# One tile for the high and the low part of x, gate and up matmuls by high weights first, and attention heads in larger units

## The chip, the cores and the metric

The kernel runs on 1 core of one Trainium2 chip. The metric is the device time of one execution in microseconds (us); lower is better. Each time given for a kernel is a median over runs. A profiled execution has a time of its own and a trace: every instruction of TensorE (PE, with its weight loads as PEld), VectorE (DVE), ScalarE (ACT) and the DMA queues, with start and duration.

## What is computed

Three transformer blocks one after the other on x of 256 tokens by 1024, all in fp32: a first block with a mixer of dilated attention and RWKV-7, then a block of two layers with a mixer of three kinds of attention. Every block or layer has a feed-forward half step before and after its mixer, so there are six of these. Cut to what the change touches:

```python
x = x + 0.5 * swiglu_2(rmsnorm(x, ffn1_norm), ffn1_w_gate, ffn1_w_up, ffn1_w_down)
h = rmsnorm(x, mix_norm) @ w_in
...
o_a = chunk_relpos_attention(hd4(a_q, A_HEADS), hd4(a_k, A_HEADS), hd4(a_v, A_HEADS), a_rel_bias)   # 6 heads of 64
o_b = dsa_attention(...)                                                                             # 5 heads of 64
o_c = mla_attention(...)                                                                             # 5 heads, q and k of 96, v of 64
x = x + jnp.concatenate([o_a, o_b, o_c], axis=-1) @ w_out
x = x + 0.5 * swiglu_2(rmsnorm(x, ffn2_norm), ffn2_w_gate, ffn2_w_up, ffn2_w_down)

def swiglu_2(x, w_gate, w_up, w_down):                    # 1024 -> 2816 -> 1024
    return (jax.nn.silu(x @ w_gate) * (x @ w_up)) @ w_down
```

## The kernel before

Nine parts run in order: f0, m1, f1 (the first block), f2, n0, f3 and f4, n1, f5 (the two layers). `f` is a feed-forward (`ffn`), `m1` the first mixer (`mixer1`), `n` a mixer of the second kind (`mixer2`).

**Numbers in two parts.** PE multiplies fp32 in a rounded form here (float32r). So that no accuracy is lost, each operand is split into a high part, which is the value rounded to that form, and a low part, which is the rest: `xh`, `xl` for x, `hi`, `lo` for weights. A product is then three matmuls: low weight by high x, high weight by high x, high weight by low x. A weight chunk of 128 by 1024 is loaded by DMA from the SP queue into `raw` (512 KB); ACT makes `hi` from it (L361), DVE makes `lo` (L362). `split` (L376, L377) does the same for other tiles.

**Feed-forward.** The 2816 hidden columns are 11 pieces of 256 (`NP`). Piece 0 has code of its own (`first`). For pieces 1 to 10, `gu(p)` computes gate and up: the weights are stationary (128 by 128), x is moving, the results are four PSUM banks of 128 by 256 (two halves `c` of gate, two of up; tags `gu`, `gu` and `tr0`, `tr1`). For each of 8 slices k of x and each of the four banks there are three matmuls of 256 columns, L557 to L559. So a group is 96 matmuls; all four banks end together at k = 7. DVE then multiplies each bank by `rrow`, the factor of the norm laid out along the columns (L565, L567), ACT takes silu (L566), DVE multiplies the two (L568), and `split` makes `hh` and `hl`. `down(p-1)` follows: 24 matmuls (L370 to L372) with `hh` or `hl` as stationary and 512 columns of the down weights as moving, into the banks y0 to y3. After group 9 no `down` stands: group 10 follows it directly.

**Heads in mixer2.** `heads` computes attention for a set of heads in units: a unit is one of the two query blocks (`qt`) with 3 or 4 heads at `qt` 0 and 1 or 2 at `qt` 1, so that a unit's scores fill one bank. A unit goes through three steps, each a step behind the unit before: `softmax` (scores by L1247, mask or bias, row maximum, exponentials with their sums), `turned` (128 by 128 transposes of the exponentials, L1265) and `values` (L1277: the transposed exponentials are stationary, 64 columns of v are moving; DVE divides by the sums, L1278 and L1279, and writes `o`). Later `ready` transposes `o` (L1420, 16 transposes in a mixer) and splits it for the output projection. There are three calls: the six heads of kind A, the five of C, the five of B. `weave` lays other work, which is mostly projections, between their steps.

**What sets the order.** The code issues instructions in the order of these loops; the framework's scheduler then lays them out per engine before the run, and each engine runs its list strictly in that order, waiting where a semaphore says so. Buffers are pools: in a feed-forward `hi`, `lo` and (from piece 2 on) `raw` have six buffers each, which six chunks a group (four of gate and up, two of down) use in turn.

Rows of the scheduled order are shown below as `line operation out<-in size`; `ps_gu`, `ps_tr0`, `ps_y` are PSUM banks by tag.

Of the kernel before, what the change touches and what calls it, by code (L numbers as in the profile page):

```python
# [9 lines left out]
F32 = mybir.dt.float32  # L10
F32R = mybir.dt.float32r
# [289 lines left out]
class Kern:  # L301
# [143 lines left out]
    def prep(self, t, gain, normed):  # L445
# [33 lines left out]
    def ffn(self, f, end):  # L479

        nc, tc = self.nc, self.tc
        with tc.tile_pool(name="ffn%d" % f, bufs=2, reuse_waits="tile") as pool:
            t2 = lambda name: pool.tile([128, 512], F32, name=name, tag="t2", bufs=12)
            self.begin(pool, t2, "f%d" % f)
            xh, xl = self.xh, self.xl
            y, hT, wd = [], [None] * NP, [None] * NP
# [15 lines left out]
            def first():  # L502
# [4 lines left out]
                for t in range(2):  # L507
# [11 lines left out]
                    nc.vector.scalar_tensor_tensor(h, ps[t][:, 256:], rs, sg, op0=OP.mult, op1=OP.mult)  # L519
# [25 lines left out]
            def gu(p):  # L545

                mm = nc.tensor.matmul
                ps = [[self.bank(tag)[:, :256] for tag in tags]
                      for tags in (("gu", "gu"), ("y2", "y3") if p == 1 else ("tr0", "tr1"))]
# [21 lines left out]
            hs, rrow = first(), []  # L571
            for p in range(1, NP):
# [7 lines left out]
            for t in range(2):  # L580
# [652 lines left out]
    def heads(self, tt, groups, qk, scores, scale, vap, o, h0, tags=("y0", "y1"), tags2=("y2", "y3")):  # L1233
# [3 lines left out]
        units = [(qt, g[i:i + 4 // (qt + 1)]) for qt in range(2) for g in groups  # L1237
# [326 lines left out]
```

## Time and profile before

| | |
|---|---|
| time, median of 3 runs | 1838.87 us (1837.1 to 1839.02) |
| the profiled execution's own time | 1841.12 us |
| its span, from first to last instruction | 1839.3 us |
| PE busy | 1819.5 us (99%) |
| PEld busy (weight loads, beside the matmuls) | 1660.0 us (90%) |
| DVE busy | 1214.9 us (66%) |
| ACT busy | 918.8 us (50%) |
| DMA | 302.53 MB, mean 164 GB/s |

Busy times of PE hold a trap: a matmul's duration in the trace goes from its start until its last result is written, and the next one starts long before that. How fast PE really goes through a list is read from starts: the start of one row to the start of the next. Shares of busy time say which engine is never without work; they do not say what an instruction costs.

### The profile page before, as it was taken

To read this page: it belongs to the slowest core of one execution; us is meant where nothing else is said; L and a number is where in the kernel's file an instruction comes from. 1 tells how busy PE (TensorE), PEld (TensorE's weight loads), DVE (VectorE), ACT (ScalarE), POOL (GpSimd) and SP (SyncE) were. 2 spreads that over 40 slices of the span, in tenths; PEclk is the share of its full clock that TensorE was granted. 3 is DMA by queue.
4 is the path that set the end of the run, shared out by engine and by line. 5 is a ranking of instruction groups with operands and counts; after the bars stand their busy time and mean duration, and the time that the engine had idled before them with its cause. 6 is when DMAs were issued, how large, how long until landed. Compare 5 with 4: busy or idle time off the path is not lost.

```text
span 1839.3 us, 31177 instructions
## 1 busy us (share of the span) xinstructions
PE 1819.5 (99%) x12404; PEld 1660.0 (90%) x12404; DVE 1214.9 (66%) x2214; ACT 918.8 (50%) x1535; POOL 0.2 (0%) x4
## 2 busy tenths in 40 slices
PE   8999999999999999999999999999999999999998
PEld 6999887999998999999998888999899988979997
DVE  6656668955667765585568667656666667666565
ACT  5544476542244544364435766444454446755443
POOL 0000000000000000000000000000000000000000
PEclk9999999999999999999999999999999999999999
DMA  8754335450146856286524337763575434347551
GB/s 273 268 185 135 121 128 142 132 160 19 35 144 200 304 196 190 74 291 200 188 74 137 121 122 260 240 187 116 200 244 179 142 104 136 119 148 250 185 182 47
DMA packets 103076, 302.53 MB, mean 164 GB/s; under 512 B 24721, under 2 KB 26897, under 8 KB 102930
## 3 DMA queue, kind: packets, MB, share of 16 engines
q1 hardware_dynamic: 102210, 298.37, 49.9%
q8 instruction: 97, 1.59, 0.3%
q10 hardware_dynamic: 720, 2.16, 0.3%
q14 instruction: 49, 0.40, 0.1%
HBM read 298.40 MB, written 2.10 MB: 163 GB/s over the span
## 4 chain that ended last, share of the span: by engine, by line
PE 96%; DVE 2%; ACT 1%; DMA 1%; issue 1%; ACTq 0%; DVEq 0%
PE ps_y L370 8%; PE ps_y L371 8%; PE ps_y L372 8%; PE ps_gu L557 6%; PE ps_gu L559 6%; PE ps_gu L558 6%; PE ps_tr L557 6%; PE ps_tr L558 6%; PE ps_tr L559 6%; PE ps_gu L370 4%; PE ps_gu L372 4%; PE ps_gu L371 4%; PE ps_gu L615 3%; PE ps_gu L617 3%; PE ps_gu L616 3%; PE ps_y L1247 1%
## 5 line engine op out<-in xcount | busy, mean ns | idle before, releaser
L362 DVE TENSOR_TENSOR lo<-raw,hi 128x1024 fp32r<-128x1024 f32 (+3 forms) x559 | 661.3, 1195 | 386.6 <-ACT hi L361 384.8
L361 ACT ACTIVATE hi<-raw 128x1024 fp32r<-128x1024 f32 (+3 forms) x559 | 568.2, 1032 | 420.2 <-PE ps_tr L559 167.4
L557 PE MATMUL ps_gu<-xh,lo 128*128 128x256 f32 x960 | 272.6, 284 | 0.4 <-DVE lo L362 0.4
L559 PE MATMUL ps_gu<-xl,hi 128*128 128x256 f32 x960 | 271.6, 283 | 0.0
L558 PE MATMUL ps_gu<-xh,hi 128*128 128x256 f32 x960 | 271.6, 283 | 0.0
L557 PE MATMUL ps_tr<-xh,lo 128*128 128x256 f32 x864 | 244.5, 283 | 0.0
L558 PE MATMUL ps_tr<-xh,hi 128*128 128x256 f32 x864 | 244.5, 283 | 0.0
L559 PE MATMUL ps_tr<-xl,hi 128*128 128x256 f32 x864 | 244.5, 283 | 0.0
L370 PE MATMUL ps_y<-lo,hh 128*128 128x512 f32 x528 | 206.5, 391 | 0.0
L372 PE MATMUL ps_y<-hi,hl 128*128 128x512 f32 x528 | 206.1, 390 | 0.3 <-DVE hl L377 0.3
L371 PE MATMUL ps_y<-hi,hh 128*128 128x512 f32 x528 | 206.1, 390 | 0.0
L557 PEld LDWEIGHTS ps_gu<-xh,lo 128*128 128x128 f32 x960 | 184.0, 192 | 3.6 <-DVE lo L362 0.8
L558 PEld LDWEIGHTS ps_gu<-xh,hi 128*128 128x128 f32 x960 | 184.0, 192 | 2.1
L559 PEld LDWEIGHTS ps_gu<-xl,hi 128*128 128x128 f32 x960 | 184.0, 192 | 0.0
L559 PEld LDWEIGHTS ps_tr<-xl,hi 128*128 128x128 f32 x864 | 165.9, 192 | 0.0
L558 PEld LDWEIGHTS ps_tr<-xh,hi 128*128 128x128 f32 x864 | 165.9, 192 | 0.0
L557 PEld LDWEIGHTS ps_tr<-xh,lo 128*128 128x128 f32 x864 | 165.9, 192 | 0.0
L372 PEld LDWEIGHTS ps_y<-hi,hl 128*128 128x128 f32 x528 | 99.1, 188 | 21.6 <-DVE hl L377 0.7
L370 PE MATMUL ps_gu<-lo,xh 128*128 128x384 f32 (+3 forms) x336 | 116.6, 347 | 0.0
L370 PEld LDWEIGHTS ps_y<-lo,hh 128*128 128x128 f32 x528 | 99.4, 188 | 18.8
L371 PEld LDWEIGHTS ps_y<-hi,hh 128*128 128x128 f32 x528 | 99.3, 188 | 18.5
L372 PE MATMUL ps_gu<-hi,xl 128*128 128x384 f32 (+3 forms) x336 | 113.0, 336 | 0.2 <-DVE xl L377 0.2
(406 smaller groups left out, 3136.8 us busy)
## 6 DMA issues: line engine op xcount, KB each, us to landing
raw<-in_w SPq DMA_DIRECT2D x492, 512.0 KB, 4.1
raw<-in_w SPq DMA_DIRECT2D x32, 384.0 KB, 3.2
raw<-in_w SPq DMA_DIRECT2D x14, 480.0 KB, 3.6
row<-in_norms SPq DMA_DIRECT2D x24, 256.0 KB, 6.8
raw<-in_w SPq DMA_DIRECT2D x10, 320.0 KB, 2.8
raw<-in_w SPq DMA_DIRECT2D x4, 492.0 KB, 6.0
raw<-in_w ACTq DMA_DIRECT2D x3, 512.0 KB, 6.9
bm<-in_bias SPq DMA_DIRECT2D x2, 768.0 KB, 5.6
```

The costliest lines, as they stand in the source:

```text
L361: nc.scalar.activation(hi[:, :w], raw[:, :w], AF.Copy)
L362: nc.vector.tensor_tensor(lo[:, :w], raw[:, :w], hi[:, :w].bitcast(F32), op=OP.subtract)
L370: mm(out, ah, bl, start=start, stop=False)
L371: mm(out, ah, bh, start=False, stop=False)
L372: mm(out, al, bh, start=False, stop=stop)
L557: mm(ps[i][c], wl[:, s], xh[:, k], start=k == 0, stop=False)
L558: mm(ps[i][c], wh[:, s], xh[:, k], start=False, stop=False)
L559: mm(ps[i][c], wh[:, s], xl[:, k], start=False, stop=k == 7)
L615: mm(ps, wl[:, s], xh, start=start, stop=False)
L616: mm(ps, wh[:, s], xh, start=False, stop=False)
L617: mm(ps, wh[:, s], xl, start=False, stop=stop)
L1247: T.matmul(ps[:, j], q[:, qt * 128:qt * 128 + 128], k[:, :nk], start=True, stop=True)
```

## The change

It has three parts.

1. `xh` and `xl` become the two halves of one tile `xx`, so that for a slice k both lie side by side as 512 columns (`x2`).
2. In `gu`, one matmul of 512 columns (L560 of the changed kernel) takes the place of the two with the high weights; it fills the whole bank, high x on the left and low x on the right. All 32 of these come first; then, bank by bank, eight matmuls of 256 columns with the low weights (L569) are added to the left half. As soon as a bank is through, ACT copies its right half out (L571) and DVE adds the left one (L572). The factor `rrow` now multiplies gate alone (L574); up stays without it, and `down`'s result gets the factor per token with the 0.5 instead (`half`).
3. In `heads`, units hold up to six heads. Even heads' scores go to one bank and odd heads' to another, issued in turn. The exponentials are divided by their sums before the transposes (a reciprocal, then one DVE instruction a head, L1285 and L1287). `values` has v as stationary (64 columns) and the transposed exponentials as moving (128 columns), so that the result is already transposed, two heads to a bank column (partitions 0 to 63 and 64 to 127). It is split straight into `mh` and `ml`; `o`, its DVE multiply and `ready` are gone.

```diff
-            self.xh = self.cst.tile([128, 8, 256], F32R, name="xh")
-            self.xl = self.cst.tile([128, 8, 256], F32R, name="xl")
+            self.xx = self.cst.tile([128, 8, 2, 256], F32R, name="xx")
+            self.xh, self.xl = self.xx[:, :, 0], self.xx[:, :, 1]
...
+            x2 = self.xx.rearrange("p k m t -> p k (m t)")
...
-                    nc.vector.scalar_tensor_tensor(h, ps[t][:, 256:], rs, sg, op0=OP.mult, op1=OP.mult)
+                    nc.vector.tensor_tensor(h, ps[t][:, 256:], sg, op=OP.mult)
...
+                low = []
                 for k in range(8):
                     if k % 2 == 0:
                         wh, wl = self.chunk(("gu", f, p, k // 2), pool, deep=pool if p > 1 else None)
+                        low.append(wl)
                     for i in range(2):
                         for c in range(2):
                             o = (k % 2) * 512 + i * 256 + c * 128
-                            s = slice(o, o + 128)
-                            mm(ps[i][c], wl[:, s], xh[:, k], start=k == 0, stop=False)
-                            mm(ps[i][c], wh[:, s], xh[:, k], start=False, stop=False)
-                            mm(ps[i][c], wh[:, s], xl[:, k], start=False, stop=k == 7)
+                            nc.tensor.matmul(ps[i][c], wh[:, o:o + 128], x2[:, k], start=k == 0, stop=False)
...
                 for c in range(2):
                     g, u = (pool.tile([128, 256], F32, name=n) for n in ("g", "u"))
-                    nc.vector.tensor_tensor(g, ps[0][c], rrow[0], op=OP.mult)
-                    nc.scalar.activation(g, g, AF.Silu)
-                    nc.vector.tensor_tensor(u, ps[1][c], rrow[0], op=OP.mult)
+                    for z, i in ((g, 0), (u, 1)):
+                        for k in range(8):
+                            o = (k % 2) * 512 + i * 256 + c * 128
+                            nc.tensor.matmul(ps[i][c][:, :256], low[k // 2][:, o:o + 128], xh[:, k], start=False,
+                                             stop=k == 7)
+                        nc.scalar.activation(z, ps[i][c][:, 256:], AF.Copy)
+                        nc.vector.tensor_tensor(z, ps[i][c][:, :256], z, op=OP.add)
+                        if z is g:
+                            nc.vector.tensor_tensor(g, g, rrow[0], op=OP.mult)
+                            nc.scalar.activation(g, g, AF.Silu)
                     nc.vector.tensor_tensor(u, u, g, op=OP.mult)
                     self.split(hh[:, c], hl[:, c], u)
...
+            nc.vector.tensor_scalar(half, self.rs, 0.5, None, op0=OP.mult)
...
-                    nc.vector.scalar_tensor_tensor(self.x[:, t, s], y[t][h], 0.5, self.x[:, t, s],
+                    nc.vector.scalar_tensor_tensor(self.x[:, t, s], y[t][h], half[:, t:t + 1], self.x[:, t, s],
...
+            for j in range(max(map(len, sides))):
+                for e in range(2):
+                    if j < len(sides[e]):
+                        q, k = qk(sides[e][j])
+                        T.matmul(ps[e][:, j], q[:, qt * 128:qt * 128 + 128], k[:, :nk], start=True, stop=True)
...
+            V.reciprocal(st[:, 1, :n], st[:, 1, :n])
+            for j in range(n):
+                V.tensor_scalar(sb[:, j], sb[:, j], st[:, 1, j:j + 1], None, op0=OP.mult)
...
+                    for h in mine:
+                        r = slice(odd(h) * 64, odd(h) * 64 + 64)
+                        T.matmul(ps[r, x], vap(kt, h), pt[:, order.index(h) * (qt + 1) + kt], start=kt == 0, stop=kt == qt)
...
+                self.split(mh[r0:r1, y:y + n, qs], ml[r0:r1, y:y + n, qs], ps[r0:r1, x:x + n])
...
-            weave(self.heads(tt, [[0, 2, 4], [1, 3, 5]], halves(aT), sc_a, 1.0, v_of(z["av"]), o, 0), fill, 1, 2, 1)
+            weave(self.heads(tt, [(0, [0, 1, 2, 3, 4, 5]), (1, [0, 1, 2, 3]), (1, [4, 5])], halves(aT), sc_a, 1.0,
+                             v_of(z["av"]), 0, at, mh, ml), fill, 1, 2, 1)
```

The calls for C and B change in the same way: units of five heads, four and one. Three places of the scheduled order follow.

PE, in the first feed-forward, at the start of group 10 before (1824 to 1827 are its four banks):

```order
L557 MATMUL ps_gu_1824<-xh_83,lo_1831 128x256
L558 MATMUL ps_gu_1824<-xh_83,hi_1830 128x256
L559 MATMUL ps_gu_1824<-xl_84,hi_1830 128x256
L557 MATMUL ps_tr0_1826<-xh_83,lo_1831 128x256
L558 MATMUL ps_tr0_1826<-xh_83,hi_1830 128x256
L559 MATMUL ps_tr0_1826<-xl_84,hi_1830 128x256
```

PE, a whole group of the changed kernel, its last slice k of the high weights and then the low ones:

```order
L560 MATMUL ps_gu<-xx,hi 128x512 x2
L560 MATMUL ps_tr_409<-xx,hi 128x512
L560 MATMUL ps_tr_410<-xx,hi 128x512
L569 MATMUL ps_gu<-xx,lo 128x256 x8
L569 MATMUL ps_tr_409<-xx,lo 128x256 x8
L569 MATMUL ps_gu<-xx,lo 128x256 x8
L569 MATMUL ps_tr_410<-xx,lo 128x256 x8
L370 MATMUL ps_y_367<-lo,hh 128x512
```

What moved: three matmuls a bank and slice became two, and the low ones, which led each slice, now end the group bank by bank.

DVE, in the first feed-forward, the end of group 9 before (1678 to 1681 are its four banks; `lo_1975` is a low tile of a chunk that comes after):

```order
L565 TENSOR_TENSOR g_1804<-ps_gu_1678,rrow_342 128x256
L567 TENSOR_TENSOR u_1805<-ps_tr0_1680,rrow_342 128x256
L565 TENSOR_TENSOR g_1812<-ps_gu_1679,rrow_342 128x256
L568 TENSOR_TENSOR u_1805<-u_1805,g_1804 128x256
L567 TENSOR_TENSOR u_1813<-ps_tr1_1681,rrow_342 128x256
L362 TENSOR_TENSOR lo_1975<-raw_1972,hi_1974 128x1024
L377 TENSOR_TENSOR hl_1803<-u_1805,hh_1802 128x256
L568 TENSOR_TENSOR u_1813<-u_1813,g_1812 128x256
```

DVE, the end of the same place in the changed kernel, where group 10 follows group 9 with no `down` between (1471 to 1474 are group 9's banks; `lo_1626` belongs to group 10 and takes the buffer of a low tile that group 9 reads until its last bank):

```order
L572 TENSOR_TENSOR g_1533<-ps_gu_1471,g_1533 128x256
L574 TENSOR_TENSOR g_1533<-g_1533,rrow_295 128x256
L572 TENSOR_TENSOR u_1534<-ps_tr0_1473,u_1534 128x256
L576 TENSOR_TENSOR u_1534<-u_1534,g_1533 128x256
L362 TENSOR_TENSOR lo_1626<-raw_1623,hi_1625 128x1024
L377 TENSOR_TENSOR hl_1532<-u_1534,hh_1531 128x256
L572 TENSOR_TENSOR g_1560<-ps_gu_1472,g_1560 128x256
L572 TENSOR_TENSOR u_1561<-ps_tr1_1474,u_1561 128x256
```

What moved: a bank is now emptied by an addition with a copy of its other half, and a weight split stands between the first two banks and the last two.

PE, in n0, the first scores of kind A and what follows until the first transpose of exponentials, before:

```order
L1247 MATMUL ps_y_11008<-qk 128x128 x3
L1247 MATMUL ps_y_11043<-qk 128x128 x3
L1374 MATMUL ps_tr_11055<-ident,cq 128x128 x2
L1247 MATMUL ps_y_11082<-qk 128x256 x2
L370 MATMUL ps_gu<-lo,c_hi 128x480
...
L1265 MATMUL ps_tr_11069<-ident,sm_s 128x128 x2
```

and now:

```order
L1264 MATMUL ps_y_10230<-qk 128x128
L1264 MATMUL ps_y_10231<-qk 128x128
...
L1414 MATMUL ps_tr_10273<-ident,cq 128x128 x2
L370 MATMUL ps_gu<-lo,c_hi 128x480
L371 MATMUL ps_gu<-hi,c_hi 128x480
L1264 MATMUL ps_y_10287<-qk 128x256 x2
L1264 MATMUL ps_y_10288<-qk 128x256
L1414 MATMUL ps_tr_10280<-ident,cq 128x128 x2
L1264 MATMUL ps_y_10288<-qk 128x256
...
L1294 MATMUL ps_tr_10325<-ident,sm_s 128x128
```

What moved: even and odd heads take turns in the first unit; in the second (256 columns) two of one side stand together, and a transpose stands before the last. Between the last score of the first unit and its first transpose stand 13 matmuls of 480 columns, six scores of 256 columns and three pairs of `cq` transposes.

## Rows read from the trace of the kernel before

**Rows 1.** The page, busy time of PE, DVE and ACT, share of the span, instructions.
```profile
PE 1819.5 (99%) x12404; PEld 1660.0 (90%) x12404; DVE 1214.9 (66%) x2214; ACT 918.8 (50%) x1535; POOL 0.2 (0%) x4
```
**Rows 2.** The page, the chain that ended last, by engine.
```profile
PE 96%; DVE 2%; ACT 1%; DMA 1%; issue 1%; ACTq 0%; DVEq 0%
```
**Rows 3.** Groups by line and form: count, busy us, mean ns, idle before.
```profile
L557 PE MATMUL ps_gu<-xh,lo 128*128 128x256 f32 x960 | 272.6, 284 | 0.4 <-DVE lo L362 0.4
```
**Rows 4.** Timeline of PE in f0: start us, duration us, engine, line, operation.
```profile
90.76 0.28 PE L559 MATMUL ps_tr<-xl,hi 128*128 128x256 f32 x1
90.88 0.40 PE L370 MATMUL ps_y<-lo,hh 128*128 128x512 f32 x1
...
91.81 0.39 PE L371 MATMUL ps_y<-hi,hh 128*128 128x512 f32 x1
...
96.12 0.39 PE L372 MATMUL ps_y<-hi,hl 128*128 128x512 f32 x1
96.34 0.28 PE L557 MATMUL ps_gu<-xh,lo 128*128 128x256 f32 x1
```
**Rows 5.** Groups by line and form: DVE and ACT in the feed-forward.
```profile
L362 DVE TENSOR_TENSOR lo<-raw,hi 128x1024 fp32r<-128x1024 f32 x495 | 599.5, 1223 | 370.2 <-ACT hi L361 368.7
L361 ACT ACTIVATE hi<-raw 128x1024 fp32r<-128x1024 f32 x495 | 513.4, 1054 | 388.8 <-PE ps_tr L559 167.4 <-issue 102.5 <-PE ps_y L372 56.3
...
L565 DVE TENSOR_TENSOR g<-ps_gu,rrow 128x256 f32<-128x256 f32 x120 | 49.9, 416 | 0.0
```
**Rows 6.** Busy time of each engine over 37 us of f0, PEclk, DMA share, GB/s.
```profile
97.00:134.00 37.00, 37.00 (x267) 35.08 (x267) 22.39 (x30) 16.67 (x22) 0.00 (x0) 1.00 0.55 176
```
**Rows 7.** Timeline of PE in n0, scores, transposes and projections.
```profile
1025.58 1.26 PE L1247 MATMUL ps_y<-qk 64*128 64x128 f32 x12
1026.77 0.44 PE L1374 MATMUL ps_tr<-ident,cq 128*128 128x128 f32 x2
1027.16 1.13 PE L1247 MATMUL ps_y<-qk 64*128 64x256 f32 x4
1028.22 0.49 PE L370 MATMUL ps_gu<-lo,c_hi 128*128 128x480 f32 x1
...
1028.54 0.38 PE L371 MATMUL ps_gu<-hi,c_hi 128*128 128x480 f32 x1
1028.76 0.38 PE L370 MATMUL ps_gu<-lo,c_hi 128*128 128x480 f32 x1
```
**Rows 8.** Timeline of PE in n0, an idle wait and the values.
```profile
1033.22 0.70 PE L1247 MATMUL ps_y<-qk 64*128 64x256 f32 x2 [0.52 <-DVE sm_s L1433]
...
1035.15 0.78 PE L1277 MATMUL ps_y<-av,sm_p 128*128 128x64 f32 x6
1035.74 0.46 PE L370 MATMUL ps_gu<-lo,c_hi 128*128 128x480 f32 x1
```
**Rows 9.** Timeline of PE in m1, an even and an odd head's scores.
```profile
333.09 0.70 PE L1128 MATMUL ps_y<-dq,qT 64*128 64x256 f32 x4
333.73 0.39 PE L615 MATMUL ps_gu<-xh,lo 128*128 128x256 f32 x1
333.95 0.28 PE L616 MATMUL ps_gu<-xh,hi 128*128 128x256 f32 x1
```
**Rows 10.** Groups by line and form: transposes of the output in both mixers n.
```profile
L1420 PE MATMUL ps_tr<-ident,o 128*128 128x128 f32 x32 | 6.6, 276 | 0.0
```
**Rows 11.** Groups by line and form, 960 to 1120 us: DVE's steps of a softmax.
```profile
L1433 DVE SCALAR_TENSOR_TENSOR sm_s<-ps_y,bm 128x384 f32<-128x384 f32 x2 | 1.1, 555 | 0.7 <-PE ps_y L1247 0.7
...
L1251 DVE TENSOR_REDUCE sm_st<-sm_s 128x3 f32<-128x384 f32 x3 | 1.6, 545 | 0.0
...
L1354 DVE TENSOR_SCALAR wk<-wk 128x128 f32<-128x128 f32 x1 | 0.2, 227 | 0.0
```
**Rows 12.** Groups by line and form, whole span: ACT's exponentials and the sums read back.
```profile
L1254 ACT ACTIVATE sm_s<-sm_s,sm_st 128x128 f32<-128x128 f32 x32 | 12.4, 391 | 1.3 <-DVE sm_st L1252 1.3
...
L1254 ACT ACTIVATION_READ_ACCUMULATOR sm_s<-sm_s,sm_st 128x1 f32 x64 | 12.2, 190 | 0.0
```

More of the change, by code (lines that the diff above doesn't have):

```diff
@@ L545, in gu @@
             def gu(p):
-                mm = nc.tensor.matmul
-                ps = [[self.bank(tag)[:, :256] for tag in tags]
+                ps = [[self.bank(tag) for tag in tags]
                       for tags in (("gu", "gu"), ("y2", "y3") if p == 1 else ("tr0", "tr1"))]
+                low = []
                 for k in range(8):
@@ L571, in ffn @@
             hs, rrow = first(), []
+            half = pool.tile([128, 2], F32, name="half", bufs=1)
+            nc.vector.tensor_scalar(half, self.rs, 0.5, None, op0=OP.mult)
             for p in range(1, NP):
@@ L1255, in softmax @@
                              accum_out=st[:, 1, j:j + 1])
-            live[i] = sb, st
+            live[i] = order, sb, st
+            yield
         def turned(i):
-            qt, g = units[i]
-            sb, st = live[i]
-            nb = len(g) * (qt + 1)
-            pT = self.bank("tr0").rearrange("p (b q) -> p b q", b=4)
-            for j in range(len(g)):
-                for kt in range(qt + 1):
-                    T.transpose(pT[:, j * (qt + 1) + kt], sb[:, j, kt * 128:kt * 128 + 128], self.ident)
@@ L1266, in turned @@
-            pt = tt("sm_p", 512, 2).rearrange("p (b q) -> p b q", b=4)
-            A.activation(pt[:, :nb], pT[:, :nb], AF.Copy)
-            live[i] = pt, st
-        def values(i):
-            qt, g = units[i]
-            pt, st = live.pop(i)
-            n, step = len(g), g[1] - g[0] if len(g) > 1 else 1
-            ps = self.bank(*tags2)[:, :n * 64].rearrange("p (h v) -> p h v", h=n)
-            for j, h in enumerate(g):
-                for kt in range(qt + 1):
-                    T.matmul(ps[:, j], pt[:, j * (qt + 1) + kt], vap(kt, h), start=kt == 0, stop=kt == qt)
-            V.reciprocal(st[:, 1, :n], st[:, 1, :n])
-            V.tensor_tensor(o[:, qt, h0 + g[0]:h0 + g[-1] + 1:step], ps,
-                            st[:, 1, :n][:, :, None].to_broadcast([128, n, 64]), op=OP.mult)
+            qt, hs = units[i]
@@ new lines, in turned @@
+            order, sb, st = live[i]
+            n = len(hs)
+            V.reciprocal(st[:, 1, :n], st[:, 1, :n])
+            for j in range(n):
+                V.tensor_scalar(sb[:, j], sb[:, j], st[:, 1, j:j + 1], None, op0=OP.mult)
+            pt = tt("sm_p", 1024, 2).rearrange("p (b q) -> p b q", b=8)
+            blocks = [(j, kt) for j in range(n) for kt in range(qt + 1)]
+            for b0 in range(0, len(blocks), 4):
+                nb = min(4, len(blocks) - b0)
+                pT = self.bank("tr0").rearrange("p (b q) -> p b q", b=4)
+                for x, (j, kt) in enumerate(blocks[b0:b0 + 4]):
+                    T.transpose(pT[:, x], sb[:, j, kt * 128:kt * 128 + 128], self.ident)
+                A.activation(pt[:, b0:b0 + nb], pT[:, :nb], AF.Copy)
+                yield
@@ new lines, in turned, with values @@
+            live[i] = order, pt
+        def values(i):
+            qt, hs = units[i]
+            order, pt = live.pop(i)
+            ms = sorted({(h0 + h) // 2 for h in hs}, key=lambda m: at[m])
+            ps = self.bank(*tags2)[:, :len(ms) * 128].rearrange("p (m q) -> p m q", q=128)
+            qs = slice(qt * 128, qt * 128 + 128)
+            rows = {}
+            for x, m in enumerate(ms):
+                mine = sorted(h for h in hs if (h0 + h) // 2 == m)
+                for kt in range(qt + 1):
+                    for h in mine:
+                        r = slice(odd(h) * 64, odd(h) * 64 + 64)
+                        T.matmul(ps[r, x], vap(kt, h), pt[:, order.index(h) * (qt + 1) + kt], start=kt == 0, stop=kt == qt)
+                r = (odd(mine[0]) * 64, odd(mine[-1]) * 64 + 64)
+                rows.setdefault(r, []).append((x, at[m]))
+                if x < len(ms) - 1:
+                    yield
+            for (r0, r1), xs in rows.items():
+                x, y, n = xs[0][0], xs[0][1], len(xs)
+                assert xs == [(x + d, y + d) for d in range(n)]
+                self.split(mh[r0:r1, y:y + n, qs], ml[r0:r1, y:y + n, qs], ps[r0:r1, x:x + n])
+            yield
@@ L1284, in heads @@
                 if 0 <= j < len(units):
[L1285 to L1286 removed]
+                    yield from f(j)
     def mixer2(self, l, end):
@@ L1304, in mixer2 @@
             V.tensor_tensor(bm, bm, chunk[:, None, :].to_broadcast([128, 6, 256]), op=OP.add)
-            o = pool.tile([128, 2, 16, 64], F32, name="o")
+            mh, ml = (pool.tile([128, 8, 256], F32R, name=n) for n in ("mh", "ml"))
+            at = {m: i for i, m in enumerate(OUT2)}
             xk = self.xk()
```

54 lines of the change are left out of this document (23 added, 31 removed).

## The prediction

> **What bounds the kernel now.** I began with the page's busy times: PE has work 99% of the span, DVE 66%, ACT 50% [rows 1]. The chain that ended last is PE for 96% [rows 2]. So the end is set by how long PE takes to go through its list, and a saving elsewhere is worth nothing unless PE waits for it. The next view, groups by line and form, gives a 256-column matmul of gate and up 284 ns [rows 3]; the timeline gives a 512-column one 390 ns [rows 4]. Those durations are latency. The pace is read from starts: 256-column matmuls stand 0.120 us apart (90.76 to 90.88), and 24 matmuls of 512 columns go from 90.88 to 96.34, which is 5.46 us or 0.2275 each [rows 4]. Twice the columns cost 0.2275, two separate matmuls 0.240. The difference, 0.0125 us, is the whole ground of the change's largest part. It could not be seen in the durations, by which a merge would seem to save 2 x 284 - 390 = 178 ns.
>
> **Gate and up.** A group is 96 matmuls before, 96 x 0.120 = 11.52 us, and then `down`, 5.46 us [rows 4]. Now it is 32 of 512 columns, 32 x 0.2275 = 7.28, and 32 of 256, 32 x 0.120 = 3.84, in all 11.12 us. I take `down`'s pace for L560, since it too streams 512 columns with a new 128 x 128 weight each time. That saves 0.40 us a group. Six feed-forwards with groups 1 to 10 make 60 groups: **-24.0 us**, all of it on PE's own list and so on the path.
>
> What a group needs beside that must fit into 11.12 + 5.46 = 16.58 us. DVE has six weight splits of 1.223 us (7.34), and now four additions, two multiplies by `rrow`, two of gate by up and two `hl`, each about 0.42 by the 256-column row of L565 (10 x 0.42 = 4.2): 11.5 us. ACT has six `hi` of 1.054 and four copies, two silu and two `hh` of about 0.4: 9.5 us [rows 5]. Before, 37 us of f0 held 22.39 us of DVE and 16.67 of ACT, with DMA at 55% and 176 GB/s [rows 6]; the same bytes 2.4% faster are 180 GB/s. None becomes the bound, and the chunks of a group are spread over the same 16.6 us.
>
> What moves within a group is when buffers come free. The four low tiles are now read until the last bank, so the splits of the next group cannot be made before this group ends. They are wanted only after `down` and the next group's high matmuls, 5.46 + 7.28 = 12.7 us later, and the six splits and ten small steps are 11.5 us, of which four splits and the last bank's steps stand in that stretch: about 4 x 1.22 + 2.5 = 7.4 us. The high tiles come free earlier than before, at the end of the high matmuls. The last bank's drain (a copy, an addition, the multiplies, silu, `hh` and `hl`, some 2.5 us at 0.42 a step) feeds only the `down` that stands one group later, and the banks are wanted again after 5.46 us. So I cost drain and buffers at nothing where `down` stands between two groups; without it they would cost up to 2.5 us a group.
>
> That cover is gone in one place of each feed-forward: group 10 follows group 9 directly. There, on DVE, `lo_1626` waits for group 9's last bank and stands ahead of the additions that empty the last two banks. It can start about 6 matmuls (0.7 us) before the group's end, so it ends at +0.5; `hl_1532` then ends at about +1.0, the addition to `g_1560` at +1.4 and that to `u_1561` at +1.9. PE wants the first of these banks after 6 matmuls of 512 columns, 1.36 us, and the second after 8, 1.82 us. That is a stall of about 0.2 us, six times: **+1.3 us** (bounds 0 and, with one split of 1.22 more in the way, 7.3).
>
> Splitting `rrow` off `up` and the factor `half` change one operand of an instruction that is there anyway. Sharing one tile for `xh` and `xl` costs nothing. Piece 0 keeps its code.
>
> **Heads, in both mixers n together.** Four terms, each on PE's list or in front of it.
> 1. The 32 transposes of `o` go [rows 10]. Two transposes take 1027.16 - 1026.77 = 0.39 us with the change of form at both ends [rows 7]; the steps that go are mostly in runs, so I take half of that for a single one, 0.1 each after rounding down: **-3 us** (bounds -6 and 0).
> 2. Scores by sides. An unpaired run of 256 columns, two heads or four passes, takes 1028.22 - 1027.16 = 1.06 us [rows 7]. In m1, where an even and an odd head take turns, two heads take 333.73 - 333.09 = 0.64 us [rows 9]. So a pair saves 0.42 us. With 8 pairs a mixer and two mixers the end is 16 x 0.42 = -6.7. By the scheduled order about half of the pairs are torn apart or have two of one side in a row. At 128 columns twelve passes take 1.19 us unpaired (1025.58 to 1026.77), 0.10 each [rows 7], with little to gain. I take **-2.5** (bounds -6.7 and 0).
> 3. Values. Before, 6 passes take 1035.74 - 1035.15 = 0.59 us, 0.098 each [rows 8], and there are 192. Now 64 columns are stationary and 128 moving, in column halves; the trace has no such matmul. Nearest rows: 0.10 for an unpaired 128-column score [rows 7], with the cost of changing halves up to 0.11; and, if two halves run side by side as the paired scores do (0.64 / 1.06 of the time), 0.06. So 192 times 0.06 to 0.11 is 11.5 to 21.1 against 18.8. The row after a paired run shows what entering and leaving split form costs: the first full matmul takes 333.95 - 333.73 = 0.22 us instead of 0.12 [rows 9]. The built order has 114 such changes where there were 72: 42 x 0.1 = +4.2. I take the middle of the pace, 0.085 (-2.5), and so **+1.7** (bounds -7 and +6.5).
> 4. The wait for the softmax. A unit now has six heads, not three or four. Its chain is two additions of 384 columns (2 x 0.555), a maximum over 768 (at most 2 x 0.545), six exponentials with their sums (6 x (0.391 + 0.190) = 3.49), two small steps of some 0.2 and the first division (0.227) [rows 11, 12], 6.3 us, and with one weight split of DVE in between up to 7.5. In the order, what PE has between a unit's last score and its first transpose is 13 matmuls of 480 columns at 1028.76 - 1028.54 = 0.22 us, six scores of 256 columns at 0.53 and three pairs of transposes at 0.39 [rows 7]: 7.2 us. Before, the same place waits 0.52 us once [rows 8]. So a wait of up to 1 us in each of the first and a half in each of the two other calls: about 1.75 us a mixer, **+3.5** (bounds 0 and +9). DVE also gets 32 divisions a mixer at 0.227 or more, 7 us in 145, and loses the multiplies by the reciprocal.
>
> The heads' sum is -3 - 2.5 + 1.7 + 3.5 = **-0.3 us**, with bounds about -12 and +14 if all four went one way.
>
> On term 3: after a paired run the next matmul takes 0.10 us more than its pace [rows 9], and that price is in the sum. The Trainium skill, TensorEngine Tiling (Array Packing), Key Properties, states that changing the tiling mode drains TensorE. If a drain waits out a whole matmul's latency, 0.284 against a pace of 0.120 [rows 3, 4], each change costs 0.16 and the 42 cost 6.9 instead of 4.2: the sum would be 2.7 us higher. The trace agrees that a change costs something and shows the smaller price, so the row is used.
>
> **Sum.** -24.0 + 1.3 - 0.3 = -23.0 us. The rows are of an execution of 1841.12 us with a span of 1839.3; the median of the runs is 1838.87, 0.1% less, and 0.1% of 23 us is nothing. 1838.87 - 23.0 = **1815.9 us**.
>
> **Rivals.**
> *The heads lose.* The larger units make PE wait for the softmax in every call, and split values run no faster than before: terms 3 and 4 near their upper bounds, +6.5 and +9, and scores gain nothing. Then the heads are +12 and the time is 1815.9 + 12 = 1828. For it: DVE already delays a score there [rows 8], and DVE has more to do. Against it: 13 projections stand as cover.
> *The heads gain.* Pairs run side by side throughout, no new waits: -6 to -9, 1808. For it: the pace in m1 [rows 9]. Against: the torn order.
> *The merge hardly saves anything.* If the cost of a matmul beyond its columns lay in `down`'s short first ones too: from 90.88 to 91.81 four go at 0.2325 each [rows 4], which leaves 2 x 0.120 - 0.2325 = 0.0075 us, or 14 us for 1920 merges, and 1826. Beside it, in TensorE: Matmul & The Clock Gate, Back-to-back issue gap, the Trainium skill gives columns / 2.4 + 2.5 ns for an isolated matmul. By that formula a merge saves 2.5 ns, an estimate of 4.8 us in all and a time of about 1835; the trace's 0.120 and 0.2275 us leave 12.5 ns, so it disagrees [rows 4].
> *Slower.* The drain is not hidden in the 54 places with a `down`: DVE stands at a `lo` that waits for the low buffer, with the additions queued behind it, and PE waits for its banks in every group as between 9 and 10. It decides from 0.40 us a group on; with one split of 1.22 us exposed each time it is 60 x (1.22 - 0.40) = +49, 1888 us. Against it: 5.46 us of `down` in front of the next use.
> *The change doesn't do what it says* in the heads: the scheduler tears every pair apart. Then term 2 is 0 and term 3 at most +6.5: 1823.
>
> **How the numbers follow.** The forecast, 1811 to 1822: 0.60. Heads lose, or their pairs are torn apart, 1822 to 1832: 0.19. Heads gain, 1804 to 1811: 0.11. Merge worth little, 1826 to 1836: 0.06. Slower: 0.04. For 8 in 10 the range reaches from **1807 to 1828**. A measurement of this kernel can tell about 0.2%, 3.7 us, from no change. Faster by more: 0.94; within: 0.03; slower: 0.03.
>
> **What would show it.** L560 starts 0.2275 apart and L569 0.120, a group with its `down` 16.6 us. PE idle 0.2 us between groups 9 and 10, waiting for L572, and nowhere else in a feed-forward. In the mixers, idle before the first transpose of a unit of six, put down to the divisions or the exponentials; pairs of L1264 starting almost together. It is wrong if L560 runs above 0.235, if PE waits for L572 or L362 in every group, or if a mixer's stretch is longer by over 5 us.

## The result and the profile after

| | before | after |
|---|---|---|
| time, median of 4 runs | 1838.94 us | 1816.49 us (1814.68 to 1820.49) |
| ratio to before, 95% interval | | 0.988 (0.9859 to 0.99) |
| span of the profiled execution | 1839.3 us | 1818.7 us |
| PE, matmuls | 12404 | 10452 |
| DVE, ACT busy | 66%, 50% | 69%, 56% |

The forecast was 1816 us. Single runs of one kernel differ by 3 us and more; in the traces the first matmul of group 1 in f0 starts at 24 or at 27 to 28 us, whatever the kernel. So below, parts of the program are compared in the traces, by starts of matmuls summed over a stretch, and whole traces from that first matmul on: 1811.5 us before and 1791.4 after.

The page of the changed kernel, busy time and the chain that ended last, answers to [rows 1, 2]: PE still sets the end.

```profile
PE 1794.3 (99%) x10452; PEld 1541.8 (85%) x10452; DVE 1257.1 (69%) x2336; ACT 1019.3 (56%) x1779; POOL 0.2 (0%) x4
...
PE 93%; ACT 2%; DVE 2%; DMA 1%; issue 1%; ACTq 0%; DVEq 0%
```

PE's timeline in f0 (start, duration, line, operation) answers to [rows 4]: the end of the high matmuls, the low ones, then `down`.

```profile
101.38 0.61 PE L560 MATMUL ps_gu<-xx,hi 128*128 128x512 f32 x2
101.83 0.62 PE L560 MATMUL ps_tr<-xx,hi 128*128 128x512 f32 x2
102.28 1.12 PE L569 MATMUL ps_gu<-xx,lo 128*128 128x256 f32 x8
...
106.11 0.40 PE L370 MATMUL ps_y<-lo,hh 128*128 128x512 f32 x1
106.35 0.40 PE L371 MATMUL ps_y<-hi,hh 128*128 128x512 f32 x1
...
111.47 0.40 PE L372 MATMUL ps_y<-hi,hl 128*128 128x512 f32 x1
111.70 0.62 PE L560 MATMUL ps_gu<-xx,hi 128*128 128x512 f32 x2
```

Two merged matmuls take 101.83 - 101.38 = 0.45 us, 0.226 each; the 32 low ones 106.11 - 102.28 = 3.83, 0.120 each. That is the pace forecast. But `down`, which the change doesn't touch, goes from 106.11 to 111.70: 5.59 us where [rows 4] have 5.46.

Over the whole trace:

| stretch or group | before, us | after, us | difference | forecast |
|---|---|---|---|---|
| gate and up (L557 to L559; L560, L569) | 692.3 | 671.3 | -21.1 | -24.0 + 1.3 |
| `down`, 1583 matmuls | 362.5 | 370.0 | +7.5 | 0 |
| n0 and n1 together | 356.2 | 351.1 | -5.2 | -0.3 |

A mixer's stretch goes from the end of group 10 before it to the first matmul of group 1 behind it, so the mixers' stretches hold 0.6 us of the +7.5. The median came out within 1 us of the forecast, but not by the right terms: the feed-forward was about 9 us worse and the heads 5 us better. The traces differ by 20.1 us where 23.0 were forecast; what is left to the medians' 22.5 is scatter of the runs.

The changed kernel's waits of PE (line waiting, engine and line waited for, us in all, times, longest) show what is new:

```profile
PE ps_tr L533 <- DVE h L520: 2.0, 2, 1.0
PE ps_gu L370 <- ACT c_hi L1419: 1.4, 2, 0.7
...
PE ps_tr L1294 <- ACT sm_p L1295: 1.1, 2, 0.6
...
PE ps_tr L1294 <- DVE sm_s L1287: 0.2, 1, 0.2
```

L533 is the transpose of piece 0 inside group 1; the other three stand in the mixers, where the kernel before waits 1.0 us for L1433 (one of the two is in [rows 8]).

### The profile page after: what moved, and what is told of

Its sections match the earlier page's. It is cut to its first block, busy times and chain, and to the rows that moved or that the text cites. A ratio compares the mean times of both kernels' runs of the same rounds, so it can differ in the third digit from the quotient of the medians.

```text
span 1818.7 us, 27775 instructions
## 1 busy us (share of the span) xinstructions
PE 1794.3 (99%) x10452; PEld 1541.8 (85%) x10452; DVE 1257.1 (69%) x2336; ACT 1019.3 (56%) x1779; POOL 0.2 (0%) x4
## 4 chain that ended last, share of the span: by engine, by line
PE 93%; ACT 2%; DVE 2%; DMA 1%; issue 1%; ACTq 0%; DVEq 0%
PE ps_gu L560 12%; PE ps_tr L560 11%; PE ps_y L370 8%; PE ps_y L371 8%; PE ps_y L372 8%; PE ps_gu L569 6%; PE ps_tr L569 6%; PE ps_gu L370 4%; PE ps_gu L372 4%; PE ps_gu L371 4%; PE ps_gu L625 3%; PE ps_gu L627 3%; PE ps_gu L626 3%; PE ps_y L930 1%; DMA raw<-in_w 1%; PE ps_y L1311 1%
## 5 line engine op out<-in xcount | busy, mean ns | idle before, releaser
L362 DVE TENSOR_TENSOR lo<-raw,hi 128x1024 fp32r<-128x1024 f32 (+2 forms) x559 | 658.7, 1193 | 77.7 <-ACT hi L361 75.8
L560 PE MATMUL ps_gu<-xx,hi 128*128 128x512 f32 x960 | 298.6, 390 | 0.7
L560 PE MATMUL ps_tr<-xx,hi 128*128 128x512 f32 x864 | 268.0, 389 | 0.0
L572 DVE TENSOR_TENSOR g<-ps_gu,g 128x256 f32<-128x256 f32 x120 | 50.6, 421 | 284.1 <-ACT g L571 284.0
L560 PEld LDWEIGHTS ps_gu<-xx,hi 128*128 128x128 f32 x960 | 179.6, 188 | 40.3 <-issue 3.1
L560 PEld LDWEIGHTS ps_tr<-xx,hi 128*128 128x128 f32 x864 | 162.2, 188 | 33.8
L569 PE MATMUL ps_gu<-xx,lo 128*128 128x256 f32 x960 | 134.8, 283 | 0.0
L569 PEld LDWEIGHTS ps_gu<-xx,lo 128*128 128x128 f32 x960 | 127.4, 191 | 4.7
L569 PE MATMUL ps_tr<-xx,lo 128*128 128x256 f32 x864 | 121.2, 283 | 0.0
L370 PE MATMUL ps_gu<-lo,xx 128*128 128x384 f32 (+3 forms) x336 | 116.1, 346 | 0.0
L372 PE MATMUL ps_gu<-hi,xx 128*128 128x384 f32 (+3 forms) x336 | 112.8, 336 | 0.3 <-DVE xx L377 0.3
L371 PE MATMUL ps_gu<-hi,xx 128*128 128x384 f32 (+3 forms) x336 | 112.5, 335 | 0.0
L569 PEld LDWEIGHTS ps_tr<-xx,lo 128*128 128x128 f32 x864 | 111.5, 192 | 0.0
L625 PE MATMUL ps_gu<-xx,lo 128*128 128x256 f32 x344 | 102.0, 297 | 1.2 <-ACT gate L1018 1.2
```

What stands on the lines that cost most here:

```text
L362: nc.vector.tensor_tensor(lo[:, :w], raw[:, :w], hi[:, :w].bitcast(F32), op=OP.subtract)
L370: mm(out, ah, bl, start=start, stop=False)
L371: mm(out, ah, bh, start=False, stop=False)
L372: mm(out, al, bh, start=False, stop=stop)
L560: nc.tensor.matmul(ps[i][c], wh[:, o:o + 128], x2[:, k], start=k == 0, stop=False)
L569: nc.tensor.matmul(ps[i][c][:, :256], low[k // 2][:, o:o + 128], xh[:, k], start=False, stop=k == 7)
```

## The experiments

Each ratio is to the kernel before, timed beside the run.

### Each part alone

```diff
 ffn_only:   before + the hunks on xx, gu, half and L517
 heads_only: before + the hunks on heads and mixer2
```

> Only the feed-forward part of the change and the shared tile; heads, values and output of both second mixers as before. By the traces' stretches the feed-forward part is worth -16 us and the rest of the program about +0.5: 1823.5 us, ratio 0.9916. The prediction's own steps for it were -24 + 1.3 = -22.7, 1816 us. Rival: the waits of 1.0 us in front of L533's transposes in f3 and f5 belong to the heads part; without it they go and the time is 1821.

> Only the heads part; feed-forward as before. By the stretches of the two traces the mixers are 2.8 and 2.4 us shorter: 1833.8 us, ratio 0.9972. The prediction's step for it was -0.3 us, 1838.6. Rival: part of the gain comes from f3's and f5's start, which waits later in the changed kernel; then less than 4 us are left, over 1835.

Measured: feed-forward alone 1824.59 us, ratio 0.9924 (0.9912 to 0.9937); heads alone 1832.28, 0.9967 (0.9955 to 0.9979). From the first matmul of group 1 they save 14.3 and 6.1 us, both together 20.1: the parts add up. The feed-forward is worth well below the 22.7 us of its steps, the heads are no draw, and the rival that left them under 4 us falls. With the feed-forward part alone, groups 1 to 10 of the six feed-forwards take as long as in the changed kernel (943.3 and 943.2 us), and PE still waits 1.8 us at L533, so that new wait belongs to the feed-forward part and not to the heads; that rival falls too.

### Why `down` became slower

Two causes stood open: what DVE and ACT do beside `down` now, or where its operands lie. `half` is a new tile of 8 bytes a partition, and everything that the pool lays out behind it moves by 32 bytes, hh and hl too, which are `down`'s stationary tiles.

```diff
 shift32, on the kernel before:
             hs, rrow = first(), []
+            half = pool.tile([128, 2], F32, name="half", bufs=1)
+            nc.vector.tensor_scalar(half, self.rs, 0.5, None, op0=OP.mult)
 half64, on the changed kernel:
-            half = pool.tile([128, 2], F32, name="half", bufs=1)
+            half = pool.tile([128, 16], F32, name="half", bufs=1)[:, :2]
```

> The kernel before with one tile of 8 bytes a partition, and the small DVE instruction that fills it, added at the same place of the feed-forward's pool; nothing reads it. hh and hl then start 32 bytes beside a multiple of 64. Order of work, buffers and banks are those of before. Theory A: down's pace goes from 0.227 to 0.232 to 0.235, about +7 to +10 us, 1846 to 1849 us, ratio 1.004 to 1.005. Theory B: no change, 1839 us, ratio 1.000 (6 more DVE instructions of under 0.1 us).

> The changed kernel with one edit: the small tile `half` is 64 bytes a partition wide instead of 8, so that the stationary tiles of `down`, hh and hl, which lie behind it, start on a multiple of 64 bytes again, as before the change (in the changed kernel they start 32 bytes beside one). Theory A (the address of the stationary tile sets the pace of down): the 512-column matmuls of down start 0.227 us apart instead of 0.234, 1584 of them, about 5 to 7 ns each: 7 to 10 us less than the changed kernel, 1807 to 1810 us, ratio to before 0.984. Theory B (what runs beside down now, splits and drains, slows it): pace stays 0.234, time 1816 us, ratio 0.988.

Measured: the kernel before with the idle tile took 1846.65 us, ratio 1.0044 (1.0032 to 1.0056). `down`'s 1583 matmuls take 370.3 us instead of 362.5. Its order of work is that of before, so theory B falls. But half64 took 1820.44, 0.99 (0.9887 to 0.9912), with `down` at 370.7 us: my theory that a multiple of 64 bytes is enough fell too. The timelines of the two, `down` in f0, first shift32, then half64:

```profile
106.93 0.40 PE L371 MATMUL ps_y<-hi,hh 128*128 128x512 f32 x1
...
110.67 0.40 PE L372 MATMUL ps_y<-hi,hl 128*128 128x512 f32 x1
```

```profile
106.23 0.40 PE L372 MATMUL ps_y<-hi,hl 128*128 128x512 f32 x1
...
106.93 0.39 PE L372 MATMUL ps_y<-hi,hl 128*128 128x512 f32 x1
```

In shift32 sixteen steps take 3.74 us, 0.234 each; in half64 three take 0.70, 0.233 each.

Three more places followed, all on the changed kernel. `half` 128 and 512 bytes wide, and `half` of 8 bytes allocated only after group 1, so that hh and hl lie where they lay before.

```diff
 half128 and half512:
-            half = pool.tile([128, 2], F32, name="half", bufs=1)
+            half = pool.tile([128, 32], F32, name="half", bufs=1)[:, :2]     (512: [128, 128])
 half_late:
                 gu(p)
+                if p == 1:
+                    half = pool.tile([128, 2], F32, name="half", bufs=1)
+                    nc.vector.tensor_scalar(half, self.rs, 0.5, None, op0=OP.mult)
```

> The changed kernel with `half` 128 bytes a partition wide: hh and hl lie 128 bytes further than in the kernel before. Theory A in the form that is left (the pace of down hangs on where the stationary tile starts, and 64 bytes are not enough): on a multiple of 128 again, so 0.227 us apart and 7 to 8 us less than the changed kernel, 1809 us, ratio 0.984. Rival A2 (what counts is that hh lies just where it lay before, for example against the moving tiles): 0.234 still, 1816 to 1820, ratio 0.988 to 0.990. Rival B (the schedule beside down) gives the same as A2 here, but cannot give the shift32 run.

> The changed kernel with `half` (8 bytes, as it was) allocated after group 1 instead of ahead of it, so that hh, hl, g and u lie at the addresses of the kernel before and nothing else changes but the place of one small DVE instruction. A and A2: down 0.227 us apart, 7 to 8 us less than the changed kernel, about 1809 us, ratio 0.984. B: 0.234, 1816 us.

> The changed kernel with `half` 512 bytes a partition wide: hh and hl move by 512 bytes against the kernel before, so that their place within 512 bytes is the old one (384), while every absolute address has changed. Theory A3 (the place within 512 bytes decides): down 0.227 us apart, about 1811 us, ratio 0.985, as half_late. Rival A2 (only the very old address gives the fast pace): 0.232 to 0.235, 1818 us, ratio 0.989.

| kernel | hh and hl start, bytes within 512 | `down`, us | time, us | ratio (95%) |
|---|---|---|---|---|
| before | 384 | 362.5 | 1838.94 | |
| changed, shift32 | 416 | 370.0, 370.3 | 1816.49, 1846.65 | 0.988, 1.0044 |
| half64 | 448 | 370.7 | 1820.44 | 0.99 |
| half128 | 0 | 368.9 | 1817.78 | 0.9893 (0.9878 to 0.9908) |
| half_late | 384 | 361.8 | 1811.25 | 0.9847 (0.983 to 0.9863) |
| half512 | 384 | 361.8 | 1810.08 | 0.9834 (0.9817 to 0.9852) |

PE's timeline of half512, `down` in f0:

```profile
106.84 0.39 PE L372 MATMUL ps_y<-hi,hl 128*128 128x512 f32 x1
107.06 0.39 PE L370 MATMUL ps_y<-lo,hh 128*128 128x512 f32 x1
...
110.24 0.39 PE L372 MATMUL ps_y<-hi,hl 128*128 128x512 f32 x1
```

Fifteen steps take 3.40 us, 0.227 each. half512 moves every tile behind `half` and has the fast pace, so it isn't the absolute address (A2 falls). From the ninth matmul of a run on, a step of `down` takes 0.227 us on the mean at 384 and 0.232 to 0.234 at the three other places.

Not only hh and hl move with `half`: so do g, u, `rrow` and `raw`. half_late has `raw` at 416 and is fast. And where no instruction of DVE or ACT has touched g, u, hh or hl for 2 us, the median step of `down` is still 0.235 us in the changed kernel (230 steps) against 0.227 before (247). So it is the place of the stationary tile.

The same traces hold other places, in matmuls of 512 columns whose moving tiles start at 128 within 512 bytes like those of `down`. In the changed kernel, m1's output projection has its stationary tiles at 256, that of the mixers n (`mh`, `ml`) at 288, and x (`xx`) at 128, as have the weights of L560. PE's timelines in m1 and at the end of n0:

```profile
562.57 0.39 PE L371 MATMUL ps_gu<-hi,mh 128*128 128x512 f32 x1
...
571.86 0.40 PE L372 MATMUL ps_gu<-hi,ml 128*128 128x512 f32 x1
```

```profile
1100.93 0.40 PE L370 MATMUL ps_y<-lo,mh 128*128 128x512 f32 x1
...
1102.81 0.39 PE L372 MATMUL ps_y<-hi,ml 128*128 128x512 f32 x1
...
1104.89 0.39 PE L372 MATMUL ps_y<-hi,xx 128*128 128x512 f32 x1
...
1106.25 0.39 PE L372 MATMUL ps_y<-hi,xx 128*128 128x512 f32 x1
```

At 256 forty steps take 9.29 us, 0.232 each; at 288 eight take 1.88, 0.235 each; and at 128, later in the same run, six take 1.36, 0.227 each. So 128 and 384 are fast, and 0, 256, 288, 416 and 448 are slow. What the slow ones collide with, and whether the place of the moving tile counts too, is not shown: no run moved it.

### Is it the merge, or all high ones first?

```diff
 merge_inter:
                             nc.tensor.matmul(ps[i][c], wh[:, o:o + 128], x2[:, k], start=k == 0, stop=False)
+                            nc.tensor.matmul(ps[i][c][:, :256], wl[:, o:o + 128], xh[:, k], start=False, stop=k == 7)
 merge_slice: the low one in a loop of its own behind the four merged ones of slice k
 both: the loop of low matmuls at the end of the group is gone
```

> The changed kernel with the low weights' matmuls not at the end of a group but each right behind the merged one of its slice: the merge alone, without all high ones first. The four banks end together. If the pace is the same wherever a 256-column matmul stands (0.2275 + 0.120), the gain of the merge stays; the low tiles come free during the group, so the wait between groups 9 and 10 of 0.28 us goes, but the drain of four banks at once takes its place there (DVE 10 steps of 0.42): within 3 us of the changed kernel, 1814 to 1820. Rival: mixing two widths costs 0.01 us or more a change, 2 x 1920 x 0.005 = +19 us, and high first is what makes the merge pay: 1835.

> The changed kernel with the low matmuls slice by slice: four merged ones of 512 columns, then four low ones of 256, so 16 changes of width a group instead of 2 (all high first) or 64 (alternating, merge_inter, where a group's gate and up took 6.6 us more over the kernel than with high first, against 2 us of waits that went). If every change costs the same, 9 us / 62 changes and 60 groups each, this one loses 14/62 of it: 2 us more than the changed kernel, less the 1.7 us of waits between groups 9 and 10: 1816 to 1819 in time. Rival: what counts is whether a run of 512-column matmuls is long enough to reach its pace (some eight after a start): then four at a time stay above 0.23 and it is as slow as merge_inter, L560 at 0.236.

Measured: 1826.61 us, 0.9933 (0.9918 to 0.9948), and 1823.37, 0.991 (0.9896 to 0.9925). Neither has a wait between groups 9 and 10 of the changed kernel's kind, and still both are slower (by 6.4 and 3.1 us from the first matmul of group 1 on). merge_inter's timeline in f0:

```profile
100.28 0.40 PE L560 MATMUL ps_tr<-xx,hi 128*128 128x512 f32 x1
100.53 0.28 PE L561 MATMUL ps_tr<-xx,lo 128*128 128x256 f32 x1
100.64 0.40 PE L560 MATMUL ps_tr<-xx,hi 128*128 128x512 f32 x1
100.88 0.28 PE L561 MATMUL ps_tr<-xx,lo 128*128 128x256 f32 x1
101.00 0.40 PE L560 MATMUL ps_gu<-xx,hi 128*128 128x512 f32 x1
```

A merged one takes 0.24 (100.64 to 100.88) where it takes 0.226 in a run, its low one 0.117 on the mean. Gate and up together: 677.8 us alternating, 672.6 in fours, 671.3 all high first, of which 3.7 are waits (1.7 at group 10, 2.0 at L533). So of about 25 us that the merge can give, all high first delivers all, runs of four some 20, alternating some 14.5. L560's mean pace is 0.236, 0.232 and, without the waits, 0.228: the longer the run the closer to 0.227. In merge_slice `down` also takes 2.1 us more; why is open. Both theories had a share of the truth: the cost isn't the same for each change (62 changes 10 us, 14 changes 5), and a run of four gets part of the pace.

### What shortened the heads

```diff
 scores_seq:
-            for j in range(max(map(len, sides))):
-                for e in range(2):
-                    if j < len(sides[e]):
+            for e in range(2):
+                for j in range(len(sides[e])):
 values_seq: in values, all even heads of the unit first, then all odd ones
```

> The changed kernel with the scores of the even heads all ahead of those of the odd heads instead of in turn; the number of matmuls is the same. If the pairs run side by side and that is where the scores' 4.6 us come from (23.55 to 18.91 us over both mixers), they go back to about 23.5 us and the time is +4 to +5 us, 1821 us. Rival: the scores became shorter because fewer changes of form stand around them in units of six; then they stay near 19 us, 1816.

> The changed kernel with the values of a unit's even heads all ahead of those of its odd heads, so that no two of different column halves follow each other. If two halves running side by side are what made values shorter (19.67 to 17.03 us over both mixers, where the prediction had +1.7), they go to 192 x 0.105 to 0.112, 20 to 21.5 us, and the time is 3 to 4 us more than the changed kernel, 1820. Rival: the smaller stationary (64 columns) alone makes them shorter, or the changes of half cost as much as running side by side gives: then within 1 us of 17.

Sums over both mixers, in us by starts (a pass is one row of the trace; each product of the heads stands there as two):

| | before | after | scores_seq | values_seq |
|---|---|---|---|---|
| scores, 128 passes | 23.6 | 18.9 | 21.0 | 18.6 |
| transposes of exponentials, 96 | 9.9 | 8.7 | 9.2 | 8.8 |
| values, 192 | 19.7 | 17.0 | 17.1 | 22.6 |
| transposes of `o`, 32 | 2.5 | gone | gone | gone |

scores_seq took 1819.84 us, 0.9899 (0.9884 to 0.9914). Taking turns gives 2.1 of the 4.6 us; the rest remains without it. That it comes from fewer and larger units, with 28 runs of scores instead of 38, is likely but has no run of its own. My expectation of the whole 4.6 was too high, and its mixers are 1.4 us longer, not 4 to 5 (PE's waits for c_hi are 0.5 us there instead of 1.4). values_seq took 1822.81, 0.9907 (0.9892 to 0.9922): values go from 17.0 to 22.6 us and both mixers are 4.6 us longer. (From the first matmul of group 1 the whole is only 1.9 us longer, because the waits at L533 happen to be missing: gate and up take 668.8 us.) The timelines of the values of kind A, in the changed kernel, then in values_seq:

```profile
1037.18 1.09 PE L1311 MATMUL ps_y<-sm_p,av 128*64 128x128 f32 x14
1038.20 0.42 PE L370 MATMUL ps_gu<-lo,xx 128*128 128x320 f32 x1
```

```profile
1038.70 1.52 PE L1311 MATMUL ps_y<-sm_p,av 128*64 128x128 f32 x16
1040.15 0.41 PE L370 MATMUL ps_gu<-lo,xx 128*128 128x320 f32 x1
```

In turn a pass takes 1.02 / 14 = 0.073 us, one side after the other 1.45 / 16 = 0.091, against 0.098 of the old form [rows 8]. The Trainium skill, TensorEngine Tiling (Array Packing), Key Properties, states that different tiles can load weights and multiply in parallel; the 0.073 against 0.091 agrees.

A short group pays for its ends, and one of them stands on another row. In the changed kernel:

```profile
1034.03 0.28 PE L371 MATMUL ps_gu<-hi,c_hi 128*128 128x256 f32 x1
1034.15 0.28 PE L372 MATMUL ps_gu<-hi,c_lo 128*128 128x256 f32 x1
1034.36 0.43 PE L1311 MATMUL ps_y<-sm_p,av 128*64 128x128 f32 x2
1034.72 0.44 PE L1294 MATMUL ps_tr<-ident,sm_s 128*128 128x128 f32 x2
```

The two passes take 0.36 us, 0.18 each, and the projection ahead of them takes 0.21 instead of 0.12. Over both mixers 20 groups of values follow a projection, and these 20 projections take 2.0 us more than their pace; before the change it was 0.1. The sums of the table leave that out.

### A version with the address mended

```diff
 late_mid, on half_late:
-MID = 5
+MID = 7
         (mixer2)
-            cols = pool.tile([128, self.I["cols"].shape[1]], F32, name="cols")
+            cols = pool.tile([128, 128], F32, name="cols")[:, :self.I["cols"].shape[1]]
```

> half_late with two more edits meant to be faster: piece 0's transposes after slice 7 of group 1 instead of 5 (MID), since PE waits 0.3 to 1.4 us for L520 in front of them in three feed-forwards of the changed kernel; and the tile cols of the mixers padded to 512 bytes, so that mh and ml start at 384 within 512 bytes, where hh does in the kernel before. From half_late's 1811: waits -2.2, output projections -0.5: 1808 us, ratio 0.983. Rival: the row of the norm's factor now comes later, DVE waits for it with group 1's additions behind, and the wait only moves: 1811.

Measured: 1807.75 us, ratio 0.9827 (0.9812 to 0.9843), the lowest median of all; the intervals of half512 and half_late overlap it. From the first matmul of group 1: 1780.1 us against 1784.0 for half_late. PE doesn't wait in front of the transposes of piece 0 any more, where half_late waited 3.0 us and the changed kernel 1.0 at a time. The same place in f3, changed kernel, then late_mid:

```profile
1120.52 0.61 PE L560 MATMUL ps_gu<-xx,hi 128*128 128x512 f32 x2
1122.13 0.44 PE L533 MATMUL ps_tr<-ident,h 128*128 128x128 f32 x2 [1.00 <-DVE h L520]
```

```profile
1113.76 0.61 PE L560 MATMUL ps_y<-xx,hi 128*128 128x512 f32 x2
1114.35 0.80 PE L533 MATMUL ps_tr<-ident,h 128*128 128x128 f32 x4
```

Gate and up go from 671.3 to 668.5 us, where 1920 x (0.2275 + 0.120) = 667.2 is the bare pace. What is left above it is no more than the wait at group 10 (0.27 us, six times); the one at L533 has not moved elsewhere. The mixers are 1.1 us shorter, but most of that is `down` at their start; their output projections went from 49.1 to 48.8 us, where 0.5 less was expected. The padding does what it should in a long run: with mh and ml at 384 instead of 288, a step from the ninth matmul of a run on takes 0.227 to 0.228 us on the mean, where it took 0.233 to 0.234. n0's end in late_mid:

```profile
1093.58 0.39 PE L370 MATMUL ps_y<-lo,mh 128*128 128x512 f32 x1
...
1094.95 0.39 PE L370 MATMUL ps_y<-lo,xx 128*128 128x512 f32 x1
```

Six steps take 1.37 us, 0.228 each. But only 30 of the 192 matmuls stand so far into a run, so the padding gives next to nothing.

## Why the prediction was right, and where not

**The merge: right in pace and size.** The pace of L560 was taken from `down`'s row, and without the waits the 60 groups give 692.3 - 667.6 = 24.7 us against 24.0. That is 0.0129 us a merge against the 0.0125 taken, so the rival with 0.0075 falls. Reading starts and not durations made the step. The prediction did not see that it rests on the second half of the change: its 0.2275 holds in a run, and alternating would have given 14.5.

**Groups 9 to 10: right.** The forecast had `lo_1626` and `hl_1532` ahead of the additions and a stall of 0.2 us. DVE and PE there in f0:

```profile
172.46 1.22 DVE L362 TENSOR_TENSOR lo<-raw,hi 128x1024 fp32r<-128x1024 f32 x1
173.60 0.42 DVE L377 TENSOR_TENSOR hl<-u,hh 128x256 fp32r<-128x256 f32 x1
173.93 0.42 DVE L572 TENSOR_TENSOR g<-ps_gu,g 128x256 f32<-128x256 f32 x1
174.27 0.41 DVE L572 TENSOR_TENSOR u<-ps_tr,u 128x256 f32<-128x256 f32 x1
```

```profile
174.00 0.39 PE L560 MATMUL ps_tr<-xx,hi 128*128 128x512 f32 x1
174.50 0.70 PE L560 MATMUL ps_gu<-xx,hi 128*128 128x512 f32 x2
```

PE stands from 174.23 to 174.50 until the addition that ends at 174.35 frees its bank: 0.275 us, six times 1.65 against 1.3. (PE's waits above count only time after the matmul before has ended, here at 174.39, and don't list so short a one.) Elsewhere drain and buffers are hidden, as costed at nothing.

**"The factor `half` costs nothing": the step that failed.** The operand costs nothing, but the tile moved hh and hl by 32 bytes, from a fast place to a slow one, and `down` lost 7.5 us. The step counted instructions and never looked at what a new tile does to the layout. No rival named it.

**Piece 0 "keeps its code": 2.0 us mis-sized.** Its transposes stand behind six slices of group 1. These take 6 x 0.907 = 5.4 us now and took 8.6, so PE arrives 3.2 us sooner at a DVE result that comes about when it came (up to 7.2 us after the start of group 1 before, up to 8.0 now).

**Heads: sum wrong by 5 us, most of it in the scores and the wait.** The four bounds add up to -19.7 and +15.5 us, not to the -12 and +14 written there. Transposes of `o`: -2.5 measured, -3 forecast, right. Scores: -4.6 against -2.5, within the bounds, but over half of the gain remained when the pairs were undone. Values: -2.6 on their own rows, but +1.9 on the projections in front of 20 groups and about +1 on the rows in front of the ten others, so near zero against +1.7. The passes were cheaper than the middle that I took, 17.0 / 192 = 0.089 us with the cost of leaving; the cost of entering, 0.1 each, was as charged. Softmax wait: PE's new waits for sm_p and sm_s are 1.3 us, against 1.0 for L1433 before, so about +0.3 where +3.5 was taken; a wait of 0.7 us a mixer for c_hi, right behind the now shorter scores, came instead, +1.4. The transposes of the exponentials had no term, rightly: of their -1.2, 1.0 is the old wait for L1433, which stands on their rows, and -0.2 is left. With -2.6 and +1.9 for the values these add up to -6.3 us. The mixers without `down` measured -5.8; the 0.5 between is on other rows, among them the output projections, whose stationary tiles went from 384 (`oh`, `ol`) to 288: 48.6 us before, 49.1 now.

So the time was right by luck: +9 us of unseen cost in the feed-forward met -5 in the heads, and the runs' own scatter of 3 us did the rest. No rival won. The "heads gain" case came near for the heads alone, though its conditions, pairs throughout and no new waits, did not hold; the slower case did not occur.

## What to carry to other kernels

Read PE's pace from starts, and price a merge by the row of the merged form in the kind of run where it will stand: the same matmul took 0.227 in a long run and 0.236 in turn with narrower ones. A new tile, however small, moves the tiles laid out behind it: compare the pace of code that the change does not touch, and if the pace moved, put the tile elsewhere before looking for another cause. A cost of changing form can stand on the row ahead of the new one: compare whole stretches beside the sums by line. When one part of PE's list gets shorter, look at each result that it meets in the middle of the stretch, not at the end alone.

## What was not expected of the hardware

The pace of 512-column matmuls depends on where the stationary tile starts: 0.227 us at 128 and 384 bytes within 512, 0.232 to 0.235 at 0, 256, 288, 416 and 448, with the moving tiles at 128. Whether matmuls of 256 columns depend on it too is open: no run moved the stationary tiles of those in gate and up. Also after a disturbance a run does not come back to 0.227 at once: in half128, behind the slow `down`, the first three pairs of L560 take 0.46, 0.47 and 0.46 us, single steps go between 0.224 and 0.236, and from the eighth on all are 0.226 or 0.227.

```profile
108.57 0.62 PE L560 MATMUL ps_gu<-xx,hi 128*128 128x512 f32 x2
109.03 0.63 PE L560 MATMUL ps_tr<-xx,hi 128*128 128x512 f32 x2
109.50 0.62 PE L560 MATMUL ps_gu<-xx,hi 128*128 128x512 f32 x2
109.96 0.62 PE L560 MATMUL ps_tr<-xx,hi 128*128 128x512 f32 x2
110.41 0.62 PE L560 MATMUL ps_gu<-xx,hi 128*128 128x512 f32 x2
```

Whether the slow pace at the wrong address and the slow pace in short runs have one cause stays open.
